# A two-layer retention and attention trunk: bias tables masked before they are loaded, gates turned into rows through DRAM, adaLN sums started from their bias, the first values copied whole

## The chip, the cores and the metric

One core of a Trainium2 chip runs the whole program in one launch. The metric is the device time of that core in microseconds, as the median of several executions. TensorE is called PE here, VectorE DVE, ScalarE ACT, GpSimd POOL and SyncE SP; SP issues most of the transfers.

## The reference, cut to what matters

A sequence of 512 rows of width 1024 goes through a retention layer and then an attention layer. Both layers start from a root-mean-square norm that is scaled, shifted and gated by a conditioning vector (adaLN):

```
cond = silu(c)
for i in range(2):
    mod = cond @ ada_w[i] + ada_b[i]            # 3072 sums of 1024 terms
    shift, scale, gate = split(mod, 3)
    h = rms_norm(x, norm_g[i]) * (1 + scale) + shift
    out = retention(h) if i == 0 else attention(h)
    x = x + gate * out
```

Retention multiplies its scores by a table of decays (chunk-causal, 64 rows to a chunk), attention adds a learned bias that depends on the distance, and masks the keys of later chunks. Weights and sums are float32; every product is made as three products of a high and a low part.

## The kernel before, in words

The 512 rows lie on 128 partitions in four tiles. Each projection is cut into chunks of 512 columns. A chunk is a list of units (`Chunk.units`), and `go` runs unit after unit; one unit is 12 matmuls of 128x512. Side work hangs on a counter of units (`now`): `at(u, fn)` calls `fn` once `u` units are done, and so norms, scores, softmaxes and their transposes get between the units. The framework's planner then orders each engine's instructions by a simulated timeline. Only inside `in_order` (lines 430 to 630 and 812 to 819) does the order written stay.

Opening (lines 430 to 630). The rows of x are squared and summed (`square`), `rstd_rows` makes the factor with one DVE operation and one POOL power, `norm` scales, `turn` transposes on PE, `keep` copies out. `warm` puts idle matmuls between, which write to a tile that nothing reads. `scale_sum` and `shift_sum` make the adaLN sums of one block of 128 columns on DVE (`ada_dot`, line 149), and with them `h_hi` and `h_lo` make the layer's input. `products(k, q)` are the first matmuls that count, 12 for each block of rows of the weights and each of two groups of columns. The values of head 0 gather in four PSUM tiles `acc[0, u]`; line 815 takes them out with `v_evac`, behind the end of the opening's pools, through a copy on ACT and a subtraction on DVE (`split`, lines 350 to 353).

The adaLN blocks that the opening doesn't need (layer 0's gates, all of layer 1) are loaded and summed as side work: `side_load`, `side_sum` (lines 784 to 800), from unit 4 to unit 100. After each fourth block `ada_finish` adds the bias; for a gate it also multiplies four identity matrices by the four sums on DVE, and has PE multiply each by a matrix of ones, so that the gate, which lay along the partitions, stands as a row on every partition; ACT copies it to `gates`.

Tables: `decays` (lines 700 to 704) and `bias` (lines 921 to 925) each start one transfer from POOL's queue, which reads the table of a head with a step of one element backwards from row to row, and then write zero or minus 1e30 into the corner that is masked. POOL writes that corner after the transfer has landed. POOL also does `rstd_of` (lines 139 to 145) for the queries and keys, and multiplies output weights by the gate (line 249). In the attention layer `turn` (line 878) transposes queries and keys once they are scaled.

Of the kernel before, what the change touches and what calls it, by code (L numbers as in the profile page):

```python
# [11 lines left out]
F32 = mybir.dt.float32  # L12
F32R = mybir.dt.float32r
I32 = mybir.dt.int32
AF = mybir.ActivationFunctionType
ALU = mybir.AluOpType

P = 128
# [24 lines left out]
def hybrid_trunk_kernel(  # L43
# [46 lines left out]
    kg = cp.tile([P, 1], F32, name="kg")  # L90
    nc.gpsimd.dma_start(kg, att_kg_t)
# [14 lines left out]
    kq = cp.tile([P, 1], F32, name="kq")  # L106
    nc.vector.tensor_scalar(kq, qg, kg, float(P**-0.5), ALU.mult, ALU.mult)
# [7 lines left out]
    mod = cp.tile([P, 2, 24], F32, name="mod")  # L115
    gs = cp.tile([P, 2, NK], F32, name="gs")
    sh = cp.tile([P, 2, NK], F32, name="sh")
    gates = [cp.tile([P, D], F32, name=f"gate_{i}") for i in range(2)]

# [28 lines left out]
    def ada_dot(raw, layer, block):  # L148
        return nc.vector.tensor_tensor_reduce(  # L149
            raw, raw, cond, 1.0, 0.0, ALU.mult, ALU.add, mod[:, layer, block : block + 1]  # L150
        )

    def ada_finish(layer, b0, n):

        m, b = mod[:, layer, b0 : b0 + n], bt[:, layer, b0 : b0 + n]
        if b0 < NK:
            nc.vector.tensor_tensor(sh[:, layer, b0 : b0 + n], m, b, ALU.add)
            return
        nc.vector.tensor_tensor(m, m, b, ALU.add)
        if b0 < 2 * NK:  # L160
            g0 = b0 - NK
            nc.vector.scalar_tensor_tensor(
                gs[:, layer, g0 : g0 + n], m, 1.0, ng[:, layer, g0 : g0 + n], ALU.add, ALU.mult
            )
            return

        ps = pa.tile([P, n, P], F32, tag="pa", name=f"gp_{layer}_{b0}")
        for j in range(n):
            diag = np_.tile([P, P], F32, tag="diag", name=f"diag_{layer}_{b0 + j}", bufs=2)
            nc.vector.tensor_scalar(diag, ident, m[:, j : j + 1], None, ALU.mult)  # L170
            nc.tensor.matmul(ps[:, j, :], ones, diag, start=True, stop=True)
        g0 = (b0 - 2 * NK) * P
        nc.scalar.activation(
            gates[layer][:, g0 : g0 + n * P], ps.rearrange("p a b -> p (a b)"), AF.Copy
        )
# [254 lines left out]
    with tc.tile_pool(name="st", bufs=1) as st, in_order():  # L430
# [4 lines left out]
        bt1 = st.tile([P, NK], F32, name="bt1")  # L435
        nc.gpsimd.tensor_scalar(bt1, bt[:, 0, NK : 2 * NK], 1.0, None, ALU.add)
# [64 lines left out]
        def shift_sum(k):  # L501
            nc.vector.scalar_tensor_tensor(
                gs[:, 0, k : k + 1], mod[:, 0, NK + k : NK + k + 1], bt1[:, k : k + 1],
                ng[:, 0, k : k + 1], ALU.add, ALU.mult,
            )
            ada_dot(raw[k][:, 0, :], 0, k)
            nc.gpsimd.tensor_tensor(
                sh[:, 0, k : k + 1], mod[:, 0, k : k + 1], bt[:, 0, k : k + 1], ALU.add
            )
# [59 lines left out]
        rstd_rows(3)  # L569
        warm(2)  # L570
# [6 lines left out]
        scale_sum(0)  # L577
        norm(3, 0)
        turn(3, 0)
        keep(2, 0)  # L580
# [25 lines left out]
        products(1, 0)  # L606
        for k in range(2):
            w_hi(k, 1)
            w_lo(k, 1)
        products(0, 1)  # L610
        for k in range(2, NK):
            if k + 2 < NK:
                loads(k + 2)
            scale_sum(k)
            shift_sum(k)
            w_hi(k, 0)
            w_hi(k, 1)
            h_hi(k)
            w_lo(k, 0)
            w_lo(k, 1)  # L620
            for _ in range(2):
                next(rope, None)
            h_lo(k)
            products(k - 1, 1)
            products(k, 0)
            if k == 6:
                first_g = Chunk("rg0", ret_w_in, [(ALLC, 2 * D + W2)], True, None)
                first_g.ready = {0: first_g.fetch(0)}
        first_g.cut(first_g.ready[0])
        products(NK - 1, 1)  # L630
# [9 lines left out]
    with l0:  # L640
# [59 lines left out]
        def decays(n):  # L700
            dec = rp.tile([P, S], F32, tag="dec", name=f"dec_{n}")
            nc.gpsimd.dma_start(dec, bass.AP(decay.tensor, n * 1280 + 127, [[576, 2], [-1, 64], [1, S]]))
            nc.gpsimd.memset(dec[64:128, 0:64], 0.0)
            pt[n] = dec
# [85 lines left out]
        def side_sum(layer, block):  # L790
# [8 lines left out]
            if block % 4 == 3:  # L799
                ada_finish(layer, block - 3, 4)  # L800
# [11 lines left out]
        with in_order():  # L812
            ev = v_evac(0)
            for u in range(4):
                ev(u, acc[0, u])
            first_g.ready[1] = first_g.fetch(1)
            first_g.cut(first_g.ready[1])
            for _ in rope:
                pass
# [34 lines left out]
    with ExitStack() as l1:  # L854
# [5 lines left out]
        def do_qk(b, begun=None):  # L860
# [32 lines left out]
            for i, a in enumerate((0, 2, 1, 3)):  # L893
                at(now[0] + (6 if begun else 10) + i // 2, turn, a)
# [26 lines left out]
        def bias(h):  # L921
            br = ap.tile([P, S], F32, tag="br", name=f"br_{h}", bufs=2)
            nc.gpsimd.dma_start(br, bass.AP(att_bias.tensor, h * 1280 + 127, [[576, 2], [-1, 64], [1, S]]))  # L923
            nc.gpsimd.memset(br[0:64, 448:512], NEG)
            brs[h] = br
# [120 lines left out]
def _constants():  # L1046
# [7 lines left out]
    return inv.reshape(P, 1), np.tile(np.stack(rows).astype(np.float32), (1, 2))  # L1054
# [61 lines left out]
```

## Time and profile before

| | us |
|---|---|
| median of 3 runs | 968.07 |
| lowest and highest | 968.01, 969.94 |
| the profiled execution, whole | 969.53 |
| its span, first to last instruction | 967.8 |
| PE busy in the span | 952.1 |
| DVE, ACT, POOL busy | 584.2, 385.4, 177.3 |

The profiled execution is 1.46 us above the median and 1.73 us lie outside its span. The chain of work that ended last is followed back from the last instruction: at each step to what released it, or to the instruction before it on its engine. PE has 95% of that chain. Busy time of PE is not yet work at PE's rate: the matmuls overlap, so their durations (some 390 ns) are longer than the step from one to the next (227 ns, as 12 products in 2.72 us show); a cost on PE is therefore read from the chain's pieces.

### The profile page before, as it was taken

To read this page: it belongs to the slowest core of one execution; us is meant where nothing else is said; L and a number is where in the kernel's file an instruction comes from. 1 tells how busy PE (TensorE), PEld (TensorE's weight loads), DVE (VectorE), ACT (ScalarE), POOL (GpSimd) and SP (SyncE) were. 2 spreads that over 40 slices of the span, in tenths; PEclk is the share of its full clock that TensorE was granted. 3 is DMA by queue.
4 is the path that set the end of the run, shared out by engine and by line. 5 is a ranking of instruction groups with operands and counts; after the bars stand their busy time and mean duration, and the time that the engine had idled before them with its cause. 6 is when DMAs were issued, how large, how long until landed. Compare 5 with 4: busy or idle time off the path is not lost.

```text
span 967.8 us, 11904 instructions
## 1 busy us (share of the span) xinstructions
PE 952.1 (98%) x4552; PEld 796.7 (82%) x4552; DVE 584.2 (60%) x1023; ACT 385.4 (40%) x800; POOL 177.3 (18%) x198
## 2 busy tenths in 40 slices
PE   7999999999999999999999999999999999999997
PEld 5878888888888888887888888888888888888786
DVE  5887774468545885782455567354567355556574
ACT  6444252333223234263445445234543254444441
POOL 3000210020002024502002250002610022005420
PEclk9999999999999999999999999999999999999999
DMA  9754444434462443321322313222231323213202
GB/s 355 265 183 142 135 144 162 161 109 142 153 213 83 160 158 106 128 81 29 112 88 84 94 48 110 90 92 92 99 98 55 104 81 96 90 58 99 95 1 87
DMA packets 71051, 113.35 MB, mean 117 GB/s; under 512 B 12289, under 2 KB 36881, under 8 KB 70994
## 3 DMA queue, kind: packets, MB, share of 16 engines
q1 hardware_dynamic: 58784, 104.87, 32.5%
q0 software_dynamic: 10768, 5.59, 2.1%
q10 hardware_dynamic: 1442, 2.13, 0.6%
q8 instruction: 36, 0.59, 0.3%
q14 instruction: 21, 0.17, 0.1%
HBM read 110.41 MB, written 2.10 MB: 116 GB/s over the span
## 4 chain that ended last, share of the span: by engine, by line
PE 95%; DMA 2%; POOL 1%; DVE 1%; issue 0%; ACT 0%; POOLq 0%; ACTq 0%; DVEq 0%
PE pm_aqk L259 6%; PE pm_aqk L261 6%; PE pm_aqk L260 6%; PE as L935 3%; PE ro L736 3%; PE pm_rg L267 3%; PE po_r L259 3%; PE pm_av L260 3%; PE po_r L260 3%; PE pm_av L259 3%; PE po_r L261 3%; PE pm_av L261 3%; PE pm_rg L269 3%; PE pm_rg L268 3%; PE ao L975 3%; PE pm_ag L267 3%
## 5 line engine op out<-in xcount | busy, mean ns | idle before, releaser
L259 PE MATMUL pm_aqk<-whi_aqk,hTh 128*128 128x512 f32 x256 | 102.2, 399 | 0.0
L261 PE MATMUL pm_aqk<-whi_aqk,hTl 128*128 128x512 f32 x256 | 100.5, 392 | 0.0
L260 PE MATMUL pm_aqk<-wlo_aqk,hTh 128*128 128x512 f32 x256 | 100.3, 392 | 0.0
L149 DVE CUSTOM_DVE_ANT_0 ada<-ada,cond 128x1024 f32<-128x1024 f32 x48 | 60.0, 1251 | 7.3 <-DMA ada<-in_ada_t_dram 7.1
L261 PEld LDWEIGHTS pm_aqk<-whi_aqk,hTl 128*128 128x128 f32 x256 | 48.1, 188 | 10.1
L259 PEld LDWEIGHTS pm_aqk<-whi_aqk,hTh 128*128 128x128 f32 x256 | 48.1, 188 | 9.3
L260 PEld LDWEIGHTS pm_aqk<-wlo_aqk,hTh 128*128 128x128 f32 x256 | 48.2, 188 | 9.1
L944 ACT ACTIVATE p<-p,nm 128x128 f32<-128x128 f32 (+1 forms) x64 | 35.9, 563 | 48.5 <-DVE nm L942 47.6
L251 DVE TENSOR_TENSOR wlo_aqk<-raw_aqk,whi_aqk 128x2048 fp32r<-128x2048 f32 x16 | 36.6, 2290 | 29.2 <-ACT whi_aqk L250 29.2
L873 DVE TENSOR_TENSOR qn<-pm_aqk,rs 128x512 f32<-128x512 f32 x32 | 22.1, 689 | 52.6 <-POOL rs L144 50.2
L938 DVE CUSTOM_DVE_ANT_0 p<-as,br 128x128 f32<-128x128 f32 (+1 forms) x64 | 30.6, 487 | 35.9 <-PE as L935 33.4
L267 PE MATMUL pm_rg<-hTh,whi_rg 128*128 128x512 f32 x128 | 50.2, 392 | 1.4 <-DVE vl L352 1.4
L268 PE MATMUL pm_ag<-hTl,whi_ag 128*128 128x512 f32 x128 | 51.1, 399 | 0.0
L267 PE MATMUL pm_ag<-hTh,whi_ag 128*128 128x512 f32 x128 | 51.1, 400 | 0.0
L923 POOL DMA_DIRECT2D br<-in_att_bias_dram x16 | 13.5, 841 | 204.2 <-DVE nm L942 151.9
L269 PE MATMUL pm_ag<-hTh,wlo_ag 128*128 128x512 f32 x128 | 50.8, 399 | 0.0
L259 PE MATMUL po_r<-whi_r,yh 128*128 128x512 f32 x128 | 50.2, 393 | 0.0
L260 PE MATMUL po_r<-wlo_r,yh 128*128 128x512 f32 x128 | 50.1, 391 | 0.0
L259 PE MATMUL pm_av<-whi_av,hTh 128*128 128x512 f32 x128 | 50.1, 391 | 0.0
L261 PE MATMUL po_r<-whi_r,yl 128*128 128x512 f32 x128 | 50.0, 391 | 0.0
L260 PE MATMUL pm_av<-wlo_av,hTh 128*128 128x512 f32 x128 | 50.0, 391 | 0.0
L261 PE MATMUL pm_av<-whi_av,hTl 128*128 128x512 f32 x128 | 50.0, 392 | 0.0
(231 smaller groups left out, 2543.8 us busy)
## 6 DMA issues: line engine op xcount, KB each, us to landing
ada<-in_ada_t_dram SPq DMA_DIRECT2D x32, 512.0 KB, 4.5
raw_aqk<-in_att_w_in_dram SPq DMA_DIRECT2D x32, 512.0 KB, 4.1
ada<-in_ada_t_dram SPq DMA_DIRECT2D x8, 1024.0 KB, 6.6
raw_rg<-in_ret_w_in_dram SPq DMA_DIRECT2D x8, 1024.0 KB, 5.1
raw_r<-in_ret_w_out_dram SPq DMA_DIRECT2D x8, 1024.0 KB, 4.9
raw_ag<-in_att_w_in_dram SPq DMA_DIRECT2D x8, 1024.0 KB, 5.3
raw_av<-in_att_w_in_dram SPq DMA_DIRECT2D x8, 1024.0 KB, 5.4
raw_a<-in_att_w_out_dram SPq DMA_DIRECT2D x8, 1024.0 KB, 5.0
```

What stands on the lines that cost most here:

```text
L149: return nc.vector.tensor_tensor_reduce(raw, raw, cond, 1.0, 0.0, ALU.mult, ALU.add, mod[:, layer, block : block + 1])
L251: nc.vector.tensor_tensor(lo, raw, f32(hi), ALU.subtract)
L259: nc.tensor.matmul(ps, a_h, wh[:, k, :], start=first and k == 0, stop=False)
L260: nc.tensor.matmul(ps, a_h, wl[:, k, :], start=False, stop=False)
L261: nc.tensor.matmul(ps, a_l, wh[:, k, :], start=False, stop=last and k == 3)
L267: nc.tensor.matmul(ps, wh[:, k, csl], h, start=first and k == 0, stop=False)
L268: nc.tensor.matmul(ps, wh[:, k, csl], l, start=False, stop=False)
L269: nc.tensor.matmul(ps, wl[:, k, csl], h, start=False, stop=last and k == 3)
L736: nc.tensor.matmul(ps[:, S - w :], a[:, fsl], b[:, psl], start=j == 0 and z == 0, stop=j == 3 and z == 2,)
L935: nc.tensor.matmul(ps[:, :w0], a[:, qsl], b[:, :w0], start=z == 0, stop=z == 2)
L938: nc.vector.tensor_tensor_reduce(p[:, :w], ps[:, :w], br[:, S - w :], 1.0, -3.0e38, ALU.add, ALU.max, mx)
L944: nc.scalar.activation(p[:, :w], p[:, :w], AF.Exp, bias=nm, accum_out=sm)
```

## The change

Four edits. (1) `ada_dot` starts its sum from the bias and scales it where needed, so that its result is the shift, the scale factor or the gate itself; `ada_finish` is gone, `ada_bias` makes one small product for each layer. With it go the operation on `bt1` at the opening, one DVE and one POOL operation for each block of the opening, and `kq` is made later. `scale_sum(0)` stands behind `norm(3, 0)` and `turn(3, 0)`. (2) A layer's gate goes as a column to DRAM two units after its last sum, and comes back as a row on all partitions two units later, both on SP's queue. (3) The masked corner of a decay or bias table is written first, and then two transfers bring one half of the partitions each, without the corner; the tables in DRAM are repeated four times instead of twice. (4) ACT copies the first values out of PSUM whole, into SBUF tiles that don't belong to the opening, before the last products; `split` then reads the copies. And `turn` of the first queries and keys in attention hangs two units later.

```diff
@@ -88,6 +88,7 @@
     qg = cp.tile([P, 1], F32, name="qg")
     nc.gpsimd.dma_start(qg, att_qg_t)
     kg = cp.tile([P, 1], F32, name="kg")
+    kq = cp.tile([P, 1], F32, name="kq")
     nc.gpsimd.dma_start(kg, att_kg_t)
 
     ones = cp.tile([P, P], F32, name="ones")
@@ -103,8 +104,7 @@
     with tc.high_priority():
         nc.scalar.activation(tick, tick, AF.Silu)
     nc.scalar.activation(cond[0:1, :], cond[0:1, :], AF.Silu)
-    kq = cp.tile([P, 1], F32, name="kq")
-    nc.vector.tensor_scalar(kq, qg, kg, float(P**-0.5), ALU.mult, ALU.mult)
+
 
     hT = {}
 
...
-    mod = cp.tile([P, 2, 24], F32, name="mod")
+    gm = cp.tile([P, 2, NK], F32, name="gm")
     gs = cp.tile([P, 2, NK], F32, name="gs")
     sh = cp.tile([P, 2, NK], F32, name="sh")
     gates = [cp.tile([P, D], F32, name=f"gate_{i}") for i in range(2)]
+    dp = ctx.enter_context(tc.tile_pool(name="dp", bufs=1, space=bass.MemoryType.DRAM))
+    rows_of = [dp.tile([1, D], F32, name=f"gate_row_{i}") for i in range(2)]
 
     @contextmanager
     def in_order():
@@ -145,34 +147,28 @@
         return rs
 
 
+
+    bg = cp.tile([P, 2, NK], F32, name="bg")
+
+    def ada_bias(layer):
+        nc.vector.scalar_tensor_tensor(
+            bg[:, layer], bt[:, layer, NK : 2 * NK], 1.0, ng[:, layer], ALU.add, ALU.mult
+        )
+
     def ada_dot(raw, layer, block):
-        return nc.vector.tensor_tensor_reduce(
-            raw, raw, cond, 1.0, 0.0, ALU.mult, ALU.add, mod[:, layer, block : block + 1]
-        )
-
-    def ada_finish(layer, b0, n):
-
-        m, b = mod[:, layer, b0 : b0 + n], bt[:, layer, b0 : b0 + n]
-        if b0 < NK:
-            nc.vector.tensor_tensor(sh[:, layer, b0 : b0 + n], m, b, ALU.add)
-            return
-        nc.vector.tensor_tensor(m, m, b, ALU.add)
-        if b0 < 2 * NK:
-            g0 = b0 - NK
-            nc.vector.scalar_tensor_tensor(
-                gs[:, layer, g0 : g0 + n], m, 1.0, ng[:, layer, g0 : g0 + n], ALU.add, ALU.mult
-            )
-            return
-
-        ps = pa.tile([P, n, P], F32, tag="pa", name=f"gp_{layer}_{b0}")
-        for j in range(n):
-            diag = np_.tile([P, P], F32, tag="diag", name=f"diag_{layer}_{b0 + j}", bufs=2)
-            nc.vector.tensor_scalar(diag, ident, m[:, j : j + 1], None, ALU.mult)
-            nc.tensor.matmul(ps[:, j, :], ones, diag, start=True, stop=True)
-        g0 = (b0 - 2 * NK) * P
-        nc.scalar.activation(
-            gates[layer][:, g0 : g0 + n * P], ps.rearrange("p a b -> p (a b)"), AF.Copy
-        )
+        kind, k = divmod(block, NK)
+        out = (sh, gs, gm)[kind][:, layer, k : k + 1]
+        start = bg[:, layer, k : k + 1] if kind == 1 else bt[:, layer, block : block + 1]
+        scale = ng[:, layer, k : k + 1] if kind == 1 else 1.0
+        return nc.vector.tensor_tensor_reduce(raw, raw, cond, scale, start, ALU.mult, ALU.add, out)
+
+    def gate_out(layer):
+
+        nc.sync.dma_start(rows_of[layer].rearrange("a (b p) -> (a p) b", p=P), gm[:, layer])
+
+    def gate_in(layer):
+
+        nc.sync.dma_start(gates[layer], rows_of[layer].broadcast_to([P, D]))
 
     def column_sums(blocks, name):
 
@@ -432,8 +428,6 @@
 
         wv = [[wp.tile([P, 4, 512], F32R, tag=a, name=f"{a}_rv0_{z}") for a in ("whi", "wlo")] for z in range(2)]
         wq = [[st.tile([P, 4, 512], F32R, name=f"{a}_rqk0_{z}") for a in ("whi", "wlo")] for z in range(2)]
-        bt1 = st.tile([P, NK], F32, name="bt1")
-        nc.gpsimd.tensor_scalar(bt1, bt[:, 0, NK : 2 * NK], 1.0, None, ALU.add)
         rows = ada_t[0, : 2 * D].rearrange("(g q p) k -> q p g k", g=2, q=NK)
         qk_in = ret_w_in[:, : 2 * D].rearrange("k (g c) -> k g c", g=2)
         raw, rw, hs, pair = {}, {}, {}, [None]
@@ -499,14 +493,7 @@
             ada_dot(raw[k][:, 1, :], 0, NK + k)
 
         def shift_sum(k):
-            nc.vector.scalar_tensor_tensor(
-                gs[:, 0, k : k + 1], mod[:, 0, NK + k : NK + k + 1], bt1[:, k : k + 1],
-                ng[:, 0, k : k + 1], ALU.add, ALU.mult,
-            )
             ada_dot(raw[k][:, 0, :], 0, k)
-            nc.gpsimd.tensor_tensor(
-                sh[:, 0, k : k + 1], mod[:, 0, k : k + 1], bt[:, 0, k : k + 1], ALU.add
-            )
 
         def w_hi(k, q):
             nc.scalar.activation((wv, wq)[q][k // 4][0][:, k % 4, :], rw[k][:, q, :], AF.Copy)
@@ -567,6 +554,7 @@
         square(3, 0, 2, A)
         square(3, 1, 2, V)
         rstd_rows(3)
+        ada_bias(0)
         warm(2)
         norm(2, 0)
         turn(2, 0)
@@ -574,9 +562,9 @@
             A.activation(cond[:, half * 512 : half * 512 + 512], cps[half], AF.Copy)
         keep(1, 0)
         warm(2)
-        scale_sum(0)
         norm(3, 0)
         turn(3, 0)
+        scale_sum(0)
         keep(2, 0)
         w_hi(0, 0)
         keep(3, 0)
@@ -604,6 +592,8 @@
             turn(t, 1)
             keep(t, 1)
         products(1, 0)
+        nc.vector.tensor_scalar(kq, qg, kg, float(P**-0.5), ALU.mult, ALU.mult)
+        ada_bias(1)
         for k in range(2):
             w_hi(k, 1)
             w_lo(k, 1)
@@ -623,10 +613,17 @@
             h_lo(k)
             products(k - 1, 1)
             products(k, 0)
+            if k == NK - 1:
+                first_v = []
+                for u in range(4):
+                    keep_v = np_.tile([P, 512], F32, tag="p", name=f"v_0_{u}", bufs=6)
+                    first_v.append(keep_v)
             if k == 6:
                 first_g = Chunk("rg0", ret_w_in, [(ALLC, 2 * D + W2)], True, None)
                 first_g.ready = {0: first_g.fetch(0)}
         first_g.cut(first_g.ready[0])
+        for u in range(4):
+            nc.scalar.activation(first_v[u], acc[0, u], AF.Copy)
         products(NK - 1, 1)
 
     offs = (0, 512, 896, 1152)
@@ -699,8 +696,12 @@
 
         def decays(n):
             dec = rp.tile([P, S], F32, tag="dec", name=f"dec_{n}")
-            nc.gpsimd.dma_start(dec, bass.AP(decay.tensor, n * 1280 + 127, [[576, 2], [-1, 64], [1, S]]))
             nc.gpsimd.memset(dec[64:128, 0:64], 0.0)
+            for a in range(2):
+                nc.gpsimd.dma_start(
+                    dec[64 * a : 64 * a + 64, 64 * a :],
+                    bass.AP(decay.tensor, n * 2560 + 127 + 1280 * a, [[608, 2], [-1, 32], [1, S - 64 * a]]),
+                )
             pt[n] = dec
 
         def scores(n, j):
@@ -796,8 +797,9 @@
                 tc.keep_in_program_order(nc.vector.tensor_tensor(xs[block], xs[block], raw, ALU.add))
                 return
             tc.keep_in_program_order(ada_dot(raw, layer, block))
-            if block % 4 == 3:
-                ada_finish(layer, block - 3, 4)
+            if block == 23:
+                at(now[0] + 2, gate_out, layer)
+                at(now[0] + 4, gate_in, layer)
 
         held = {}
         blocks = [(0, 16 + b) for b in range(8)]
@@ -812,7 +814,7 @@
         with in_order():
             ev = v_evac(0)
             for u in range(4):
-                ev(u, acc[0, u])
+                ev(u, first_v[u])
             first_g.ready[1] = first_g.fetch(1)
             first_g.cut(first_g.ready[1])
             for _ in rope:
@@ -891,7 +893,7 @@
                     kT[2 * b + a - 2] = (hi, lo)
 
             for i, a in enumerate((0, 2, 1, 3)):
-                at(now[0] + (6 if begun else 10) + i // 2, turn, a)
+                at(now[0] + (8 if begun else 10) + i // 2, turn, a)
             if begun:
                 begun.evac = evac
                 return begun.units((1,))
@@ -920,8 +922,12 @@
 
         def bias(h):
             br = ap.tile([P, S], F32, tag="br", name=f"br_{h}", bufs=2)
-            nc.gpsimd.dma_start(br, bass.AP(att_bias.tensor, h * 1280 + 127, [[576, 2], [-1, 64], [1, S]]))
             nc.gpsimd.memset(br[0:64, 448:512], NEG)
+            for a, w in ((0, 448), (1, 512)):
+                nc.gpsimd.dma_start(
+                    br[64 * a : 64 * a + 64, :w],
+                    bass.AP(att_bias.tensor, h * 2560 + 127 + 1216 * a, [[608, 2], [-1, 32], [1, w]]),
+                )
             brs[h] = br
 
         def softmax(h, i):
...
```

## Rows read from the trace of the kernel before

**Rows 1.** The page, busy time of each engine

```profile
PE 952.1 (98%) x4552; PEld 796.7 (82%) x4552; DVE 584.2 (60%) x1023; ACT 385.4 (40%) x800; POOL 177.3 (18%) x198
```

**Rows 2.** Waits of PE: who for whom, us in all, times, longest

```profile
PE hp L483 <- DVE xn L475: 3.2, 1, 3.2
PE qt L881 <- DVE qn L873: 2.4, 3, 1.8
PE pm_rg L267 <- DVE vl L352: 1.4, 1, 1.4
```

**Rows 3.** Chain of work, 10 to 21 us: start, us, what

```profile
10.82 1.12 PE hp L483 x4
11.93 0.85 PE idle L494 x2
...
16.99 3.20 PE idle L494 x14
```

**Rows 4.** Timeline, 0 to 21 us: start, us, engine, line [idle before <-releaser]

```profile
4.63 1.06 ACT L464 ACTIVATE xT<-x 128x1024 f32<-128x1024 f32 x1 [0.89 <-DMA x<-in_x_dram]
7.55 1.06 ACT L464 ACTIVATE xT<-x 128x1024 f32<-128x1024 f32 x1 [1.77 <-DMA x<-in_x_dram]
8.05 0.25 POOL L436 TENSOR_SCALAR bt<-bt 128x8 f32<-128x8 f32 x1 [4.43 <-DMA bt<-in_ada_bt_dram]
8.39 0.21 DVE L107 TENSOR_SCALAR kq<-qg,kg 128x1 f32<-128x1 f32 x1 [7.14 <-DMA kg<-in_att_kg_t_dram]
8.58 1.21 DVE L466 CUSTOM_DVE_ANT_0 xT<-x 128x1024 f32<-128x1024 f32 x1
```

**Rows 5.** Chain of work, 455 to 465 us

```profile
447.85 8.11 DMA br<-in_att_bias_dram
...
457.56 1.05 POOL rs L144
...
461.68 0.43 PE pm_ag L267
```

**Rows 6.** Stretches: us, busy by engine (instructions), granted clock, DMA share, GB/s

```profile
10.80:16.80 6.00, 5.98 (x23) 4.95 (x23) 4.49 (x12) 3.79 (x8) 3.14 (x5) 1.00 1.05 408
...
460.50:463.90 3.40, 3.40 (x13) 2.92 (x12) 3.40 (x5) 1.77 (x3) 0.00 (x0) 0.51 0.35 69
```

**Rows 7.** DVE's instructions by line and shape: busy us, mean ns | idle before

```profile
L149 DVE CUSTOM_DVE_ANT_0 ada<-ada,cond 128x1024 f32<-128x1024 f32 x48 | 60.0, 1251 | 7.3 <-DMA ada<-in_ada_t_dram 7.1 <-ACT cond L574 0.2
```

**Rows 8.** Timeline, 56 to 80 us

```profile
65.56 2.07 ACT L351 ACTIVATE vh<-pm_rv 128x512 fp32r<-128x512 f32 x4 [4.07 <-PE pm_rqk L540]
...
66.19 2.48 DVE L352 TENSOR_TENSOR vl<-pm_rv,vh 128x512 fp32r<-128x512 f32 x4 [2.37 <-ACT vh L351]
66.94 0.50 PE L267 MATMUL pm_rg<-hTh,whi_rg 128*128 128x512 f32 x1 [1.41 <-DVE vl L352]
```

**Rows 9.** Chain of work, 117 to 125 us

```profile
124.33 0.44 PE gp L171 x4
```

**Rows 10.** Tile gp: its matmuls, duration ns min/median/max

```profile
L171 PE MATMUL gp<-diag,ones x32: 270/274/275, 117.8 to 404.0; 128*128 128x128 f32 x32
```

**Rows 11.** DMA issues: count, KB each, us to landing

```profile
qg<-in_att_qg_t_dram POOLq DMA_DIRECT2D x1, 0.5 KB, 5.7
```

**Rows 12.** Timeline of SP and of ACT: weights issued, and first read

```profile
129.27 0.38 SPq L243 DMA_DIRECT2D raw_rv<-in_ret_w_in_dram  x1
...
149.97 1.91 ACT L250 ACTIVATE whi_rv<-raw_rv 128x2048 fp32r<-128x2048 f32 x1
...
405.96 0.37 SPq L243 DMA_DIRECT2D raw_ag<-in_att_w_in_dram  x1
...
426.41 1.94 ACT L250 ACTIVATE whi_ag<-raw_ag 128x2048 fp32r<-128x2048 f32 x1
```

**Rows 13.** Tiles br and raw_a: POOL's issues and products, ns min/median/max

```profile
L923 POOL DMA_DIRECT2D br<-in_att_bias_dram x16: 787/853/869, 447.8 to 892.0; - x16
...
L249 POOL TENSOR_TENSOR raw_a<-raw_a,gate x32: 1276/1293/3362, 554.2 to 925.5; 128x512 f32<-128x512 f32 x32
```

More of the change, by code (lines that the diff above doesn't have):

```diff
@@ L1053, in _constants @@
         rows.append(np.exp(np.float64(lg) * dist) * 256.0**-0.5)
-    return inv.reshape(P, 1), np.tile(np.stack(rows).astype(np.float32), (1, 2))
+    return inv.reshape(P, 1), np.tile(np.stack(rows).astype(np.float32), (1, 4))
 _INV_FREQ_HEX = """
@@ L1079 @@
     bias = np.concatenate(
-        [np.broadcast_to(rel[:, 256:], (AH, 383)), rel[:, 256:0:-1], rel[:, 0:1]] * 2, axis=1
+        [np.broadcast_to(rel[:, 256:], (AH, 383)), rel[:, 256:0:-1], rel[:, 0:1]] * 4, axis=1
     )
```

## The prediction, made before the changed kernel was run

> **What bounds the kernel now.** I read the page first: PE is busy for 98% of the span, every other engine for 60% or less [rows 1]. So whatever changes the time takes matmuls off PE, or fills a hole in PE's row, or makes a new one. The second view is the waits of PE [rows 2]: five entries, of which the change touches three, together 7.0 us. The reader should see how little that is: with PE full, work taken from DVE, ACT or POOL pays only where it ends one of these waits. The third view is the chain of work around each hole, for what it hangs on, and the fourth the granted clock in stretches. The changes go through in order of time.
>
> **Opening.** PE has a hole of 3.2 us before its first transposes, which wait for a DVE scaling [rows 2]; they start at 10.82 [rows 3]. Behind it stand two waits for small loads. DVE's first operation of weight is `kq`, and it stands until 8.39 for a load of 512 bytes; POOL stands until 8.05 for the bias [rows 4]. Both go. The rows that matter are there earlier: ACT begins on the first tile of x at 4.63 and on the third at 7.55, both released by their transfers, so the second lands between, at about 6.0 [rows 4]. New walk: first sum of squares done at 4.63 + 1.06 + about 0.1 for its read-out = 5.8; POOL's power some 1 us (the one at [rows 5] takes 1.05), 7.0. But DVE's order puts the square of the second tile first: 6.0 + 1.21 [rows 4] and two small operations, 7.5; the scaling takes 0.5, so the transposes start at 8.0, when PE is just done with its four broadcasts (10.82 less 3.2 is 7.6). That is 2.8 us earlier.
>
> What is late next: four groups of transposes and three pairs of idle matmuls follow on PE in a fixed order, up to 16.99, then 14 idle matmuls in 3.20 us up to 20.19, where the products begin [rows 3]. If all of it shifts, the products begin 2.8 us earlier. Two things can hold it. One is the clock: a pair of idle matmuls takes 0.85 us at 11.93 (0.43 each, the lower level, 1.2 GHz), and of the 14 each takes 0.23 (2.4 GHz) [rows 3]; the granted clock reads 1.00 all the while [rows 6], so this early the level is read from the step. If the rise stays at the same moment, the first six or seven of the 14 run at half rate and 1.3 us are given back; if it comes sooner, up to 3.3 is gained. The other is the weights: DMA moves 408 GB/s there with all its engines busy [rows 6], so nothing lands sooner. The first adaLN sum waited for the condition, not for its weights (0.2 us, [rows 7]). Each block loses a DVE and a POOL step from its path as well, which offsets a sum that starts later. The 48 sums take 1.25 us each [rows 7]; that scale and start come from memory may add something, for which no row has a price: between 0 and one small operation, 0.2 us as `kq` [rows 4], twice on the path in the opening. I take 2.7, with 1.0 and 3.3 as ends.
>
> **First values.** At 65.56 ACT takes the first values out. It had been idle for 4.07 us and was released by the last products: the target tiles take the place of the opening's, which are then still read [rows 8]. PE waits for the copy and the subtraction, 1.41 us. With four copies into tiles of another pool, which need only the products that end 12 steps of 0.227, 2.7 us, before, the four PSUM tiles are free in time: four such copies took 2.07 together [rows 8], and 2.7 is there. ACT does four copies more, 2.1 to 2.5 us; PE has 8 units, over 20 us, before the scores need what stands behind. Gain 1.5, between 1.0 and 1.6.
>
> **Gates.** Each `gp` piece costs PE 0.44 us in the chain [rows 9], and 32 matmuls in fours [rows 10] are eight pieces: 3.5 us that PE no longer does, with nothing on PE in their place. 16 DVE scalings and four ACT copies go too, hidden beside PE and worth nothing by themselves. In their place stand four transfers on SP. The gate back waits for the gate out, and SP's queue stands behind that wait. The nearest row for a transfer of four-byte pieces is `qg`: 128 of them landed in 5.7 us [rows 11]; the gate has 1024. Two units lie between the issues, 5.4 us, so SP would stand from nothing to some 10 us twice. What is queued behind: for layer 0 weights issued at 129.27 and first read at 149.97, for layer 1 weights issued at 405.96 and read at 426.41 [rows 12]: 20.5 us each, of which some 5 are the transfer. Cost 0, at worst 1 for each layer.
>
> **Tables.** POOL waits for each bias table to land before it writes the corner. Once this reaches PE: at 447.85 the tables of heads 0 and 1 are issued, POOL stands until 457, and only then makes the power that the queries need, at 457.56 [rows 5]; PE waits 1.8 of the 2.4 us in the row of `qt` [rows 2]. Then the clock falls: from 460.5 to 463.9 the granted clock is 0.51 [rows 6], and a matmul takes 0.43 instead of 0.23 [rows 5]. 13 matmuls and some transposes in 3.40 us, where full rate needs about half, cost some 1.6. With the corner first, POOL has four issues of at most 0.87 [rows 13], done by 451.4; the power follows six us earlier, and the transposes hang two units (5.4 us) later too. Both parts go: 1.8 and 1.6. The other 0.6 of `qt` stands at 912 behind gate products of POOL; 0 to 0.6, I take 0. Each table now costs a second issue, 0.5 to 0.9 us more on POOL, 20 in all; at 18% busy it hides.
>
> **Sum.** 2.7 + 1.5 + 3.5 + 1.8 + 1.6 = 11.1. Against the profiled execution's 969.53: 958.4. The median is 1.46 lower, about the price of the low-clock stretch, and the three runs lie in two places 1.9 apart; so the median may lack that stretch. Without this term it gives 968.07 - 9.5 = 958.6; with it 957.0. I forecast 958.4.
>
> **Rivals.**
> *The opening gives little*: the clock rises no sooner or the weights hold the sums, 1.0 instead of 2.7, and the holes come back in part elsewhere, since the planner orders both layers anew (1 to 2 us): 960.5 to 962. For it speaks the full DMA, against it that nothing in the opening waited for weights. Chance 0.22.
> *All ends well*: 3.3 in the opening, the 0.6 at 912, an end in which the planner's new order also closes a hole or two: 955.5. Chance 0.12.
> *The gates hold SP*: the round trip through DRAM takes over 15 us, weights come late by some 2 to 4 us in one layer, and the clock falls behind the hole (1.6): 962 to 964. The cover of 15 us in both places speaks against it. Chance 0.06.
> *Slower, by POOL*: the 16 added issues of the bias tables get in front of the powers for queries and keys. Price 0.53 to 0.87 each, 8.5 to 14 if all reach PE, and the 3.4 of the tables is then not gained: 968.07 - 7.7 + 8.5 to 14, 969 to 974. It decides from the point at which eight heads or more lose their cover. Rows against it: POOL is 82% idle, and its 7 to 8 us of waits per table go. POOL's products stretch from 1276 to 3362 ns, while its issues stay within 787 and 869 [rows 13]. Chance 0.03. The Trainium skill, SBUF — State Buffer, section "SBUF: two separate sides", says that descriptors of a transfer from GpSimd's queue can't be written while a two-port DVE operation holds the shared port, which speaks against more such transfers; by that rule the added issues would stretch too. The 16 issues here don't show it.
> *No change*: holes only move, and the opening and the tables give nothing; 3.5 of the gates stays, 1.5 to 3.5 come back as new waits: 966 to 968. Chance 0.03.
>
> **How the numbers follow.** The forecast's own case (957 to 960) has 0.54. Range 955.3 to 962.5: it takes in the low case, the opening's ends and most of the first rival. Measurement can tell some 0.2%, 2 us, from no change. Faster: 0.54 + 0.22 + 0.12 + 0.06 = 0.94; same 0.03; slower 0.03.
>
> **What would show it.** In the profile after: DVE's first square near 6 us instead of 8.58, the transposes near 8.0, the first products near 17.5 instead of 20.2; no wait of `pm_rg` near 63; no matmul on `gp`; POOL's bias issues with no wait for a landing behind them, and no low clock near 455. The prediction is wrong if the products still start at 20, if `pm_rg` or `qt` still stand in PE's waits, or if new entries over 1 us do.

## The result, and the profile after

The changed kernel takes 957.08 us (median of 4 runs, 956.84 to 957.25) beside 969.01 us for the kernel before on the same chip: a ratio of 0.9875, with an interval of 0.9858 to 0.9892. Forecast were 958.4 us and a range of 955.3 to 962.5. The profiled execution went from 969.53 to 956.93 us, 12.6 less. In 30 runs beside the first four experiments the kernel before lies between 966.55 and 971.49 us; of the changed kernel no run of these four is more than 0.41 from another.

The page's line of busy times (engine, us, share of the span, instructions), to be held against [rows 1]:

```profile
PE 945.3 (99%) x4520; PEld 790.7 (83%) x4520; DVE 580.0 (61%) x991; ACT 384.8 (40%) x800; POOL 190.3 (20%) x209
```

PE has the 32 matmuls on `gp` less. POOL has become busier by 13 us, and the kernel faster by 12: POOL's own busy time costs nothing here. The waits of PE (who for whom, us in all, times, longest):

```profile
PE cp L537 <- ACT cond L106: 4.2, 1, 4.2
PE pt L961 <- DVE p L953: 0.9, 1, 0.9
PE hp L477 <- DVE xn L469: 0.3, 1, 0.3
PE pm_rv L527 <- ACT hTh L510: 0.2, 1, 0.2
```

That is the whole list. Of the three waits of [rows 2] two are gone, `qt` and `pm_rg`, and so is the 3.2 us of `hp`; the 0.3 us of `hp` that is listed now stands before a later group of transposes, at 11.70. The first line is the start of the program; the second, at 932 us, was there before.

**Opening.** Timeline of 0 to 21 us (start, us, engine, line, [idle before <- what ended it]), against [rows 4]:

```profile
5.81 1.23 DVE L460 CUSTOM_DVE_ANT_0 xT<-x 128x1024 f32<-128x1024 f32 x1
8.06 1.12 PE L477 MATMUL hp<-ident,xn 128*128 128x128 f32 x4
9.82 1.05 PE L477 MATMUL hp<-ident,xn 128*128 128x128 f32 x4
11.70 0.66 PE L477 MATMUL hp<-ident,xn 128*128 128x128 f32 x4 [0.27 <-DVE xn L469]
13.04 3.47 PE L488 MATMUL idle<-ones_r 128*128 128x512 f32 x14
16.69 1.21 PE L527 MATMUL pm_rv<-whi_rv,hTh 128*128 128x512 f32 x4 [0.18 <-ACT hTh L510]
```

DVE's first square stands at 5.81 instead of 8.58, the transposes at 8.06 instead of 10.82, the products at 16.69 instead of 20.03. The same four transposes take 1.05 us at 9.82 and 0.66 at 11.70: PE goes over to its higher level, 2.4 GHz, in between, thus ahead of the 14 idle matmuls, while before it did so at 16.8, with the first of them. The chain of work shows what the products now wait for:

```profile
1.65 6.77 DMA x<-in_x_dram
...
13.86 1.20 DVE ada L163
...
15.16 0.82 ACT h L507
...
16.69 3.06 PE pm_rv L527 x12
```

Before, that chain ran through `kg`'s load (issued at 2.61, 5.67 us) and then over PE itself, transposes and idle matmuls in a row [rows 3, 4]. Now it runs through x's third tile, the last scaling, the adaLN sums and ACT, and PE has 0.18 us to spare.

**First values.** ACT on the timeline, 52 to 70 us, against [rows 8]:

```profile
59.00 2.07 ACT L626 ACTIVATE v<-pm_rv 128x512 f32<-128x512 f32 x4 [1.69 <-PE pm_rv L527]
62.45 2.19 ACT L347 ACTIVATE vh<-v 128x512 fp32r<-128x512 f32 x4 [1.38 <-issue]
```

The four copies lie from 59.00 to 61.07, beside the last 12 products. PE's chain there has no hole, where the product of [rows 8] stood until 66.94:

```profile
59.64 2.72 PE pm_rqk L527 x12
62.36 0.23 PE pm_rg L263
```

**Gates.** The DMA issues (out <- in, queue, count, KB each, us to landing), then SP on the timeline, 380 to 420 us:

```profile
gate<-gate_row SPq DMA_DIRECT2D x2, 512.0 KB, 5.6
gate_row<-gm SPq DMA_DIRECT2D x2, 4.0 KB, 10.3
```

```profile
384.55 0.37 SPq L167 DMA_DIRECT2D gate_row<-gm  x1
394.29 0.34 SPq L171 DMA_DIRECT2D gate<-gate_row  x1
...
397.94 0.37 SPq L239 DMA_DIRECT2D raw_ag<-in_att_w_in_dram  x1
```

The gate takes almost twice as long to get out, 4 KB in pieces of four bytes, as to come back on all partitions. SP stands between the two, with weights queued behind, and no wait of PE comes of it.

**Tables.** POOL on the timeline, 420 to 470 us, against [rows 5]:

```profile
439.01 0.15 POOL L925 MEMSET br<- 64x64 f32 x1 [1.28 <-PE pm_aqk L257]
439.32 1.41 POOL L927 DMA_DIRECT2D br<-in_att_bias_dram  x2 [0.16 <-issue]
...
440.78 1.34 POOL L927 DMA_DIRECT2D br<-in_att_bias_dram  x2
...
443.21 1.04 POOL L146 TENSOR_TENSOR rs<-ms,mhalf 128x4 f32<-128x4 f32 x1
```

Two corners and four issues in 3.1 us (all 32 issues on POOL: busy us, mean ns | idle before; then the DMA issues, KB and us to landing):

```profile
L927 POOL DMA_DIRECT2D br<-in_att_bias_dram x32 | 22.5, 706 | 2.3 <-issue 2.3
```

```profile
br<-in_att_bias_dram POOLq DMA_DIRECT2D x16, 128.0 KB, 5.8
br<-in_att_bias_dram POOLq DMA_DIRECT2D x16, 112.0 KB, 5.0
```

POOL no longer stands for a landing: the power that stood behind two landings at 457.56, 9.7 us after the first issue, is made at 443.21, 3.9 us after it. (The issues themselves come 8.5 us earlier, by what was gained ahead of them.) The granted clock is 1.00 from the opening to PE's last matmul (stretch, busy by engine, clock, DMA share, GB/s), where [rows 6] had 0.51:

```profile
17.00:953.00 936.00, 933.02 (x4480) 782.97 (x4478) 571.33 (x969) 374.23 (x782) 182.52 (x192) 1.00 0.36 116
```

### The profile page after: what moved, and what is told of

Read it like the earlier page. It is cut to its first block, busy times and chain, and to the rows that moved or that the text cites. A ratio compares the mean times of both kernels' runs of the same rounds, so it can differ in the third digit from the quotient of the medians.

```text
span 955.1 us, 11856 instructions
## 1 busy us (share of the span) xinstructions
PE 945.3 (99%) x4520; PEld 790.7 (83%) x4520; DVE 580.0 (61%) x991; ACT 384.8 (40%) x800; POOL 190.3 (20%) x209
## 4 chain that ended last, share of the span: by engine, by line
PE 98%; DMA 1%; DVE 0%; ACT 0%; issue 0%; POOL 0%; SPq 0%; ACTq 0%
PE pm_aqk L255 6%; PE pm_aqk L257 6%; PE pm_aqk L256 6%; PE as L941 3%; PE ro L737 3%; PE ao L981 3%; PE po_a L255 3%; PE pm_ag L264 3%; PE pm_ag L263 3%; PE po_r L255 3%; PE pm_rg L263 3%; PE po_a L256 3%; PE pm_ag L265 3%; PE po_a L257 3%; PE po_r L257 3%; PE pm_av L255 3%
## 5 line engine op out<-in xcount | busy, mean ns | idle before, releaser
L925 POOL MEMSET br<- 64x64 f32 x16 | 2.8, 177 | 244.1 <-DVE mx L944 143.6
L245 POOL TENSOR_TENSOR raw_a<-raw_a,gate 128x512 f32<-128x512 f32 x32 | 45.7, 1459 | 27.1 <-DMA raw_a<-in_att_w_out_dram 13.8
L264 PE MATMUL pm_rg<-hTl,whi_rg 128*128 128x512 f32 x128 | 49.8, 389 | 0.0
```

The costliest lines, as they stand in the source:

```text
L245: nc.gpsimd.tensor_tensor(raw[:, k, :], raw[:, k, :], scale, ALU.mult)
L264: nc.tensor.matmul(ps, wh[:, k, csl], l, start=False, stop=False)
```

## The experiments

### Each part alone

Four kernels are the kernel before with one part of the change. Beside them the kernel before took 967.97 us.

**Opening alone**: `kq` late, sums that begin from their bias in the opening's blocks, `scale_sum(0)` behind `turn(3, 0)`.

```diff
-    nc.vector.tensor_scalar(kq, qg, kg, float(P**-0.5), ALU.mult, ALU.mult)
...
-        nc.gpsimd.tensor_scalar(bt1, bt[:, 0, NK : 2 * NK], 1.0, None, ALU.add)
...
-        scale_sum(0)
         norm(3, 0)
         turn(3, 0)
+        scale_sum(0)
...
         products(1, 0)
+        nc.vector.tensor_scalar(kq, qg, kg, float(P**-0.5), ALU.mult, ALU.mult)
```

> Kernel before with the opening's edits alone (the two early waits gone, adaLN sums of the opening begun from their bias, the first scale sum after the last scaling); gates, tables and first values as before. Theory of separate holes: the products begin near 16.7 as in the changed kernel instead of 20.2, the holes of pm_rg (1.4) and qt (1.8) stay, the median falls by 3.0 to 3.6 us. Rival, the opening gives little because the weights or the clock hold it: 1.0 or less, products at 19 or later.

Measured: 964.96 us (9 runs, 963.0 to 966.97), ratio 0.9970 (0.9959 to 0.9981). The transposes begin at 8.08, the products at 16.36. The later waits stay:

```profile
PE qt L882 <- DVE qn L874: 2.2, 1, 2.2
PE pm_rg L267 <- DVE vl L352: 1.4, 1, 1.4
```

The matmuls of PE come in the same order as before, so nothing but the opening differs; it is worth 3.0 us by the medians, 3.7 by the start of the products. One pair of profiles says little to a tenth: in the seven with the new opening or a variant of it the products begin between 16.36 and 16.95, in the five with the old one between 19.77 and 20.37.

**First values alone**: the four tiles `v_0_u` and copies, and `ev` reads them.

```diff
+            if k == NK - 1:
+                first_v = []
+                for u in range(4):
+                    keep_v = np_.tile([P, 512], F32, tag="p", name=f"v_0_{u}", bufs=6)
+                    first_v.append(keep_v)
...
+        for u in range(4):
+            nc.scalar.activation(first_v[u], acc[0, u], AF.Copy)
...
-                ev(u, acc[0, u])
+                ev(u, first_v[u])
```

> Kernel before with the copy of the first values alone. Separate holes: the wait of pm_rg is gone, 1.3 to 1.6 us less, nothing else moves. Rival, the copies on ACT make the second half of the gate weights late: a new wait in the same place, 0 to 0.5 us less.

Measured: 966.05 us (10 runs, 965.1 to 969.3), ratio 0.9981 (0.9968 to 0.9994): 1.9. The wait of `pm_rg` is gone, `qt` waits 1.8 as before. The chain of work, 445 to 466 us, is that of [rows 5] once more, but what stands behind the hole isn't:

```profile
446.50 8.29 DMA br<-in_att_bias_dram
...
456.17 1.05 POOL rs L144
...
461.39 0.23 PE pm_ag L268
```

A matmul takes 0.23 us here, the higher level, where [rows 5] had 0.43 after a hole of the same size. Of five profiled executions with a hole there, of 1.4 to 2.2 us (before, this one, opening, gates, and the one with the later transposes below), only that of before has the low clock.

**Gates alone**: `gate_out` and `gate_in` for the eight `gp` pieces.

```diff
-            if block % 4 == 3:
+            if block == 23:
+                at(now[0] + 2, gate_out, layer)
+                at(now[0] + 4, gate_in, layer)
+            elif block % 4 == 3 and block < 2 * NK:
                 ada_finish(layer, block - 3, 4)
```

> Kernel before with the gates through DRAM alone, shift and scale as before. Separate holes: eight pieces of 0.44 us leave PE, 3.3 to 3.7 us less, and no wait of PE comes in their place although SP stands for up to 10 us before the gate comes back. Rival, SP's stand makes weights late: a new wait of PE over 1 us, 0 to 2.5 us less.

Measured: 965.49 us (10 runs, 963.12 to 967.21), ratio 0.9969 (0.9957 to 0.9981): 2.5 by the medians. The trace tells it more closely: from the first product on `pm_rg` to the start of the last matmul it is 890.3 us, and 893.8 with the first values alone. That is 3.5, and no wait of PE is new. The clock is the likely reason for the lower median: 5 of these 10 executions have a mean granted clock of 0.998 or less on record, as the profiled execution of before has. The other five have a median of 964.03, and the 23 of 30 executions of the kernel before with a mean clock above 0.998 have 967.67, 3.6 more.

**Tables alone**: the corner first, and two transfers around it.

```diff
-            nc.gpsimd.dma_start(br, bass.AP(att_bias.tensor, h * 1280 + 127, [[576, 2], [-1, 64], [1, S]]))
             nc.gpsimd.memset(br[0:64, 448:512], NEG)
+            for a, w in ((0, 448), (1, 512)):
+                nc.gpsimd.dma_start(
+                    br[64 * a : 64 * a + 64, :w],
+                    bass.AP(att_bias.tensor, h * 2560 + 127 + 1216 * a, [[608, 2], [-1, 32], [1, w]]),
+                )
```

> Kernel before with the masked tables alone; the transposes of the first queries and keys hang where they did. Theory that POOL's stand behind the two first tables makes the hole: hole and low clock near 457 are gone, 3.2 to 3.8 us less. Rival, the place of the transposes in the order makes it: the hole stays in good part, 0 to 1.5 less. Rival, the second issues on POOL cost: new waits on qn, 0 or more us added.

Measured: 964.92 us (10 runs, 964.68 to 967.17), ratio 0.9971 (0.9962 to 0.998): 3.05. The stretch from `pm_rg` to the last matmul is 891.9, thus 1.9 less. What PE waits for, beside `cp` at the start and `pt` at the end, which every kernel here has:

```profile
PE hp L483 <- DVE xn L475: 3.6, 2, 3.5
PE pm_rg L267 <- DVE vl L352: 1.4, 1, 1.4
...
```

The transposes still hang on unit 6 here, and `qt` doesn't wait. The four gains are 3.0, 1.9, 2.5 and 3.05, 10.45 together. The changed kernel ran elsewhere, beside other runs of the kernel before: 11.9 below those, 10.9 below the ones here. The four ratios multiply to 0.9891, at the edge of the 0.9858 to 0.9892 of the whole. The stretches of the trace add up more closely: 893.8 - 3.5 - 1.9 = 888.4, and the changed kernel has 888.35. So from `pm_rg` on the parts neither help nor hinder each other.

### The transposes two units later

The prediction had named two reasons for the end of the hole near 459: an earlier power, and transposes that hang two units later. One kernel is the one before with the later unit alone, the other the changed kernel with the earlier one.

```diff
-                at(now[0] + (6 if begun else 10) + i // 2, turn, a)
+                at(now[0] + (8 if begun else 10) + i // 2, turn, a)
```

> Kernel before with the first transposes of queries and keys hung two units later, tables as before. Theory that POOL's stand makes the hole and that two units (5.4 us) cover it too: power at 457.6, transposes wanted near 463, no wait on qt, 1.8 us less (and up to 1.6 more in executions in which the clock fell). Rival: POOL's stand goes on to the next power, and the hole stays: 0 to 0.5 less.

Measured: 967.94 us beside 968.99 (10 runs, 966.67 to 969.27), ratio 0.9994 (0.9984 to 1.0003), no difference, where I had expected 1.8 less. The wait has only moved:

```profile
PE pm_ag L267 <- DVE qn L873: 1.4, 1, 1.4
```

PE doesn't wait for the transposes' source now but for the PSUM tile that the late `qn` still reads. Two units are 5.4 us of other matmuls, and were no cover: the next chunk stood behind the same power.

> Changed kernel with those transposes back at their old place. Theory: the tables alone close the hole, same time within 0.3 us, no wait on qt. Rival, the tables need the two units as well: a wait on qt of 0.5 to 1.5 and as much slower.

Measured: 957.09 us (4 runs, 956.73 to 957.48), ratio 0.9883 (0.9868 to 0.9897), as the changed kernel. The tables close the hole alone.

### The two waits of the opening, one put back at a time

One kernel is the changed one with `kq` made early again, the other has the operation on `bt1` again, whose result nothing reads there.

```diff
     nc.scalar.activation(cond[0:1, :], cond[0:1, :], AF.Silu)
+    nc.vector.tensor_scalar(kq, qg, kg, float(P**-0.5), ALU.mult, ALU.mult)
...
         products(1, 0)
-        nc.vector.tensor_scalar(kq, qg, kg, float(P**-0.5), ALU.mult, ALU.mult)
```

```diff
+        nc.gpsimd.tensor_scalar(bt1, bt[:, 0, NK : 2 * NK], 1.0, None, ALU.add)
         rows = ada_t[0, : 2 * D].rearrange("(g q p) k -> q p g k", g=2, q=NK)
```

> Changed kernel with kq back ahead of DVE's first square. Theory that DVE's wait for 512 bytes sets the start of the transposes: they are back near 10.7, the products near 19 to 19.5, 2.5 to 3 us slower. Rival, the adaLN sums set the products and not the transposes: under 1 us slower.

Measured: 960.3 us (4 runs, 960.03 to 960.62), ratio 0.9916 (0.9901 to 0.9931), 3.2 more than the changed kernel. The load of `kg` landed 0.8 us later than in the kernel before, so the transposes stand at 11.60 and not near the 10.7 that I had expected. The timeline:

```profile
9.18 0.21 DVE L107 TENSOR_SCALAR kq<-qg,kg 128x1 f32<-128x1 f32 x1 [7.92 <-DMA kg<-in_att_kg_t_dram]
11.60 1.12 PE L478 MATMUL hp<-ident,xn 128*128 128x128 f32 x4 [4.03 <-DVE xn L470]
```

> Changed kernel with POOL's operation on the bias back ahead of its first power (its result is read by nothing). Theory: POOL stands to about 8.1 to 8.3, the first power ends near 9.2, transposes near 9.8 instead of 8.06, 1.0 to 1.7 us slower. Rival: PE's four broadcasts and the landing of x cover it, 0 to 0.4 slower.

Measured: 958.65 us (4 runs, 958.21 to 959.09), ratio 0.9900 (0.9884 to 0.9917), 1.6 more. Its timeline:

```profile
8.42 0.25 POOL L432 TENSOR_SCALAR bt<-bt 128x8 f32<-128x8 f32 x1 [4.82 <-DMA bt<-in_ada_bt_dram]
9.80 1.11 PE L479 MATMUL hp<-ident,xn 128*128 128x128 f32 x4 [1.77 <-DVE xn L471]
```

DVE's wait alone takes all of the opening's gain back, POOL's about half (1.6 us): the later of the two sets the start, so an edit that had removed only POOL's would have shown nothing.

### What sets the start of the products now

> Changed kernel with 6 idle matmuls instead of 14 ahead of the first products. Theory that the products now wait for their input (the adaLN sums and the step behind them) and that the idle matmuls only fill the time: products start at the same 16.5 to 16.8, PE idle about 2 us before, same time within 0.5 us. Rival, PE's own order set the start: products about 1.8 us earlier and as much faster. Second rival: the idle stretch costs clock, products run at the lower level for a while, 1 us or more slower.

```diff
-        warm(14)
+        warm(6)
```

Measured: 956.56 us (4 runs, 956.33 to 956.67), ratio 0.9886 (0.9871 to 0.9901): no difference from the changed kernel that these runs can tell, since the time is 0.5 lower, but the kernel before is 1.4 lower beside it too. The products begin at 16.53, and the eight idle matmuls that are gone are waited for instead:

```profile
PE pm_rv L527 <- ACT hTh L510: 1.3, 1, 1.3
```

So it is the data that sets the start, and not PE's order. Nor is it the clock: its rise stands at 13.01 in this profile, 2.1 us later than in the changed kernel's, and the products begin no later. The last kernel of this kind puts `scale_sum(0)` ahead of the last transposes again, with the last scaling on ACT.

```diff
         warm(2)
-        norm(3, 0)
+        scale_sum(0)
+        norm(3, 0, A)
         turn(3, 0)
-        scale_sum(0)
...
-        warm(14)
+        warm(11)
```

> Changed kernel with the first scale sum ahead of the last scaling, that scaling on ACT, and 11 idle matmuls instead of 14. Theory that the sums' path sets the first products: they start 0.2 to 0.6 us earlier, and the time falls as much. Rival, ACT becomes late with its copies: the same start or later, 0 to 0.5 us slower.

Measured: 957.28 us (4 runs, 956.82 to 957.67), ratio 0.9894 (0.9879 to 0.9909). The products begin at 16.70, as before the edit, where I had expected 0.2 to 0.6 us earlier. The chain of work begins with another load:

```profile
2.58 9.77 DMA ada<-in_ada_t_dram
...
12.51 0.58 DVE ada L163
```

The sum has gone ahead of the scaling and still starts at 12.51, since its weights land at 12.35. With both small loads out of the way the opening is held by the large ones. (A hole of 0.7 us for `pt` at 558 is new here; PE's order there is another.)

### How much more the gates and the tables bear

**Gates, three trips instead of one**, which carry the same numbers each time.

```diff
         nc.sync.dma_start(gates[layer], rows_of[layer].broadcast_to([P, D]))
+        for _ in range(2):
+            nc.sync.dma_start(rows_of[layer].rearrange("a (b p) -> (a p) b", p=P), gm[:, layer])
+            nc.sync.dma_start(gates[layer], rows_of[layer].broadcast_to([P, D]))
```

> Changed kernel with three round trips of each gate through DRAM in sequence instead of one (the same values each time). One trip takes some 16 us (10.3 out, 5.6 back), so SP stands some 32 us longer behind each layer's last sum. Theory that some 15 us of cover stood behind each trip: weights come 12 to 17 us late in both places and PE shows waits of that kind, 10 to 34 us slower. Rival, the cover is far larger: the same time within 1 us.

Measured: 979.98 us (4 runs, 979.29 to 981.28), ratio 1.0130 (1.0114 to 1.0146), 22.9 more than the changed kernel and within the 10 to 34 expected, though of the 12 to 17 us expected in each layer the first has only 4.3. PE's order is the same; its waits are new:

```profile
PE hp L218 <- DVE xn L198: 12.8, 1, 12.8
...
PE pm_rg L266 <- ACT whi_rg L249: 3.2, 1, 3.2
PE pm_rg L268 <- DVE wlo_rg L250: 1.1, 1, 1.1
```

and the chain of work of the 12.8 us, 400 to 452:

```profile
423.30 12.10 DMA gate_row<-gm
...
435.79 7.46 DMA raw_ag<-in_att_w_in_dram
...
443.34 1.92 ACT whi_ag L249
...
448.92 0.41 DVE xn L198
...
449.37 1.97 PE hp L218 x8
```

SP comes to the weights at 435.79 instead of 397.94, ACT's high part follows them, DVE's low part follows ACT, and behind it on DVE's queue stands the scaling that PE's transposes need. With the granted clock at 0.50 from 179.7 to 186.5 and from 439.1 to 452.7, where PE was busy for 5.67 and 3.33 us, half of that is lost as well: 12.8 + 3.2 + 1.1 + 4.5 = 21.6 of the 22.4 us by which the span grew. The rival *the gates hold SP* is a real mechanism; one trip stays within its cover, three don't.

**Tables, four transfers instead of two**, for bias and decays: `c` and `d` run over the columns below and above 256.

```diff
-                nc.gpsimd.dma_start(
-                    br[64 * a : 64 * a + 64, :w],
-                    bass.AP(att_bias.tensor, h * 2560 + 127 + 1216 * a, [[608, 2], [-1, 32], [1, w]]),
-                )
+                for c, d in ((0, 256), (256, w)):
+                    nc.gpsimd.dma_start(
+                        br[64 * a : 64 * a + 64, c:d],
+                        bass.AP(att_bias.tensor, h * 2560 + 127 + 1216 * a + c, [[608, 2], [-1, 32], [1, d - c]]),
+                    )
```

> Changed kernel with each table brought in four transfers instead of two (each half cut once more by columns): 40 issues more on POOL, at 0.65 to 0.88 us each some 26 to 32 us of POOL time. Theory that POOL's issues are hidden: the same time within 0.4 us, no new wait of PE on qn. Rival, POOL's issues get in front of the powers: a wait of PE for each head that loses its cover, 2 us or more in all.

Measured: 963.01 us (4 runs, 962.33 to 963.5), ratio 0.9953 (0.9936 to 0.997), 6 more than the changed kernel. I had expected it hidden; that was wrong. The groups of POOL's instructions (busy us, mean ns | idle before) and PE's new waits:

```profile
L929 POOL DMA_DIRECT2D br<-in_att_bias_dram x64 | 44.2, 709 | 2.1 <-issue 2.1
```

```profile
PE pm_ag L265 <- DVE wlo_ag L247: 3.0, 2, 1.7
...
PE ao L983 <- DVE ptl L348: 0.9, 2, 0.4
...
```

An issue costs the same 0.71 us for half the bytes, so the 32 added ones take 22 us of POOL. But none of the waits is for POOL, and at the first two bias tables, 440 us, PE has no wait behind eight issues in a row. What differs is the order: PE's matmuls, the same in order up to 449 us, stand elsewhere in 306 of 4520 places from there on. Nothing but the tables was edited, so it is the added issues that made the planner lay out PE's work anew, and the products met operands that weren't ready. With two of `po_a` (0.7) the six holes are 4.6 us. Behind each, the first step on PE is some 0.3 us longer than the others (0.50 instead of 0.23 for `pm_ag` in the chain of work), and with that they make the 6.2 us by which the stretch from `pm_rg` to the last matmul grew (888.35 to 894.55). That the order is the cause, and not the issues in themselves, is argued here and not shown: the same order with these issues wasn't tried.

## Why the prediction held, point by point

- **Opening, 2.7 between 1.0 and 3.3: under-sized, 3.3 measured** (20.03 to 16.69), the upper end. The walk over the loads was right to 0.1 us, square at 5.81 and transposes at 8.06. The upper end was tied to a clock that rises sooner, and it did. What the prediction had wrong is the path behind the transposes, "if all of it shifts": PE's fixed order was taken as the path and the clock as what could hold it. The path is now another one, x's third tile, sums, ACT, and the products begin 0.8 us before the 17.5 forecast. The rival *the opening gives little* had its weights right as the next bound, in the last kernel of the opening; they weren't the bound yet.
- **First values, 1.5: 1.4 in the trace** (46.91 us from the first product to `pm_rg`, then 45.51), 1.9 by the medians.
- **Gates, 3.5 and nothing for SP: 3.5 in the trace.** SP stood twice, 17.2 us in all, within the "nothing to some 10 twice".
- **Tables, the hole: 1.8 forecast, 1.9 in the trace.** Of the two causes one was none: the transposes' two units add nothing, alone or undone. The earlier power does it.
- **Tables, the low clock, 1.6:** there in the profiled execution of before, and in none of the four others with the hole. The mean granted clock on record for each execution says more. With the tables as before it is 0.998 or less in 23 of 89 executions (the kernel before beside the experiments, 11 of 50, and the four kernels that keep its tables); with the new tables it is so in none of 38, the three gate trips with their own holes left out. The mean doesn't tell where the clock was low, but the change removes it. So the term is real, belongs to about a quarter of the executions, and the median lacks it, as the sum had doubted; the forecast of 958.4 kept it. Its price was under-sized: the stretch from `pm_rg` to the last matmul is 896.5 us before and 893.8 with the first values alone, and of these 2.7 only some 0.6 are the other waits of `qt`, at 912. Those 0.6, of which I took 0, are gone after, but the profiles of the four kernels with one part each don't show them either, so this is one execution's evidence.
- **Second issues on POOL, hidden:** right for two transfers a table. The 32 take 0.71 us each in the mean, and the 16 of before had a median of 0.85 [rows 13]. The rival *slower, by POOL* put its price on powers that come late; the kernel with four transfers shows a price by another way, most likely through the order that the planner makes.
- **The sum.** In the profiled execution 12.6 instead of 11.1. By the traces the opening is 3.3, the first values 1.4, the gates 3.5, the hole 1.9, the low clock with the waits at 912 2.7, less 0.2 behind the last matmul: 12.6. So the 1.5 too little are the opening, the waits at 912 and the price of the low clock, some 0.5 each. By the medians it is 11 to 12, where the terms without the low clock made 9.5. The time lies 1.3 below the forecast, half of it from the opening.
- The sentence on the Trainium skill, SBUF — State Buffer, section "SBUF: two separate sides", by which added issues from GpSimd's queue would stretch under DVE's work: the 32 issues take 652 to 877 ns while DVE is 61% busy, and the 16 took 787 to 869 [rows 13]. No run here shows a stretch.

## What to carry to other kernels

Where one engine is busy for 98%, read the few waits in its row and price the change by them; work that goes from the other engines counts only there, and two waits that release the same engine must go together. Small loads at the head of an in-order queue cost far more than their bytes, and a corner that is written before the transfer around it takes a landing off a queue. A free trip or issue says nothing of the next one: count the cover, and where a planner orders the work, look at the order after each edit too.

## What was not expected of the hardware

- A sum on DVE takes longer with its start or scale from memory. Of 128x1024 elements, with constants, it took 1251 ns [rows 7]; now, by DVE's groups of instructions (mean ns):

```profile
L163 DVE CUSTOM_DVE_ANT_0 ada<-ada,cond,bt 128x1024 f32<-128x1024 f32 x32 | 42.3, 1322 | 2.4 <-DMA ada<-in_ada_t_dram 2.4
L163 DVE CUSTOM_DVE_ANT_0 ada<-ada,cond,bg 128x1024 f32<-128x1024 f32 x16 | 22.4, 1401 | 6.9 <-DMA ada<-in_ada_t_dram 6.9
```

  By these means one operand is 0.07 us, two are 0.15, within the bound of 0.2. Single instructions that took up to 2.3 us raise the means; by the medians, 1218, 1278 and 1340 ns, it is 0.06 and 0.12.
- A table of 256 KB landed in 8.2 us in one transfer, and its halves in 5.0 and 5.8, issued 0.7 us apart, thus both within 6.5; its quarters take 3.7 and 4.1. The Trainium skill, DMA: Bandwidth & Descriptors, section "Rules for kernel authors", advises against two transfers to separate halves of the partitions, since they share the same engines. Here the halves are there sooner; their reading pattern differs from that of the whole, so the split isn't the only cause that could be.
- PE's clock: its rise moved from 16.8 to 10.9 us with transposes that began 2.8 us earlier, and it isn't fixed by them. In the seven profiles with transposes from 8.0 to 8.3 us it lies between 10.9 and 13.0, in the five with the old opening between 14.5 and 16.8; with `kq` early again it is at 17.1. A hole of 1.4 to 2.2 us near 459 was followed by the lower level in one of five profiled executions, and the mean clock of all executions on record speaks for about a quarter. What decides was not settled.
